# A decoder layer on one core: the next FFN part's first gate block moves in front of the down projections

## The chip, the cores and the metric

The kernel runs on one core of one Trainium2 chip. The metric is the device time of one launch in microseconds. The engines are named as in the profile: PE (TensorE matmul) with its weight loads PEld, DVE (VectorE), ACT (ScalarE), POOL (GpSimd) and SP (SyncE, which here only issues DMAs).

## The reference

One decoder layer over 256 tokens with model width 2048, all in float32. Two token mixers (retention and RG-LRU), a gated merge, a cross-attention over 256 memory tokens, and then the part that this change concerns:

```python
def conv_gated_ffn(hn, w_up, conv_w, conv_b, w_down):
    up = causal_dwconv(hn @ w_up, conv_w, conv_b)     # w_up: 2048 x 11264, 3 taps along the tokens
    gate, val = jnp.split(up, 2, axis=-1)
    return (jax.nn.silu(gate) * val) @ w_down         # w_down: 5632 x 2048
...
hn = rmsnorm(h, norm_ffn_w[l])
h = h + conv_gated_ffn(hn, ffn_w_up[l], ffn_conv_w[l], ffn_conv_b[l], ffn_w_down[l])
return rmsnorm(h, final_norm_w)
```

## The kernel before

**Matmuls in split float32.** Every operand is the sum of a rounded part `hi` and a remainder `lo`. A weight piece of 512 x 512 (1 MB, the tile `raw`, six buffers) is loaded by a DMA that SP issues; ACT writes `hi` (line 286), DVE writes `lo` (line 287), three buffers each. Three products (hi·hi, hi·lo, lo·hi) make one. One such piece is a *unit*: `units` yields the units in the order of `weight_plan`, and prepares each two units ahead (`AHEAD`).

**Three forms of a matrix product.** `gemm_n` has the tokens on the output's partitions: per unit 24 matmuls of 512 columns (lines 362, 363, 369), four units for an inner dimension of 2048. `gemm_t` has the features on the output's partitions: per unit 16 matmuls of 512 columns and 16 of 256 (line 351). `pair_products` makes two output blocks of 512 columns at once in 11 units with sums of operands (a Strassen-like scheme): seven units `q1` to `q7` of 12 matmuls and four units `p0` to `p3` of 24, in the order q1 p0 q3 p1 q5 q2 q6 p2 q7 q4 p3. Units q5 and q7 take their weights by a DMA of POOL that adds in place. `pair_add` adds the results to the residual rows `hrow`; its `out` is called after each unit.

**Callbacks.** `later(n, fn)` runs `fn` after the unit numbered n from here (0 is the next one) in the program's order. A scheduler then places the instructions on the engines' queues by priority and by buffers that are free; an engine works off its own queue in order.

**The FFN.** The 11 feature blocks of 512 are done in three parts of 4, 4 and 3 (`FF_PARTS`). In a part each block has two products, a gate block and a value block; `up` makes one. With `at` given it takes `gemm_n` and turns the result by DMA: ACT copies the accumulator into 16-bit planes (`row_planes`, line 757), two transposing DMAs of SP turn them (`turn_planes`, line 778), and at the two steps in `at` ACT joins the planes (line 763), DVE scales (line 1301), and `conv` does the three taps (ACT line 1311, DVE line 1313). With `at` None it takes `gemm_t`, whose result needs no turning. After the value block `hidden` makes silu(gate) times value and splits it (lines 1384 to 1386, 555, 556) into the operands `hid` of the down projection. The last value block of each part is made by `gemm_t`, and its conv and `hidden` run inside the first units of the down projection that follows. The down projection of a part of four blocks is two calls of `pair_add` (columns 0 and 1, then 2 and 3); unit p2 is the first that reads the last block's `hid`.

**Space.** The pool `bp` has 24 buffers of 4 KB per partition (`big`): the eight operands `h2s` of the FFN, up to eight `hid` and four sums of them, gate and value tiles `fg` and `fv`, planes `rp` and `d`, and the residual rows. The four residual row blocks are kept in DRAM (`fkept`) while a part's up products run, and `get_rows` brings them back: blocks 0 and 1 in the last value block, 2 and 3 in the first pair of the down projection.

**rsb.** `spread_tokens` spreads the reciprocal norms over the partitions with four small matmuls (line 605); `rsb2` is first read when the first gate block of the FFN has been turned.

Of the kernel before, what the change touches and what calls it, by code (L numbers as in the profile page):

```python
# [9 lines left out]
F32 = mybir.dt.float32  # L10
# [7 lines left out]
P = 128  # L18
# [46 lines left out]
def weight_plan():  # L65

    w0 = "w_in"
    plan = []
    v, u = O_V, O_V + 1024
    plan += [(w0, 0, NT, O_Q), (w0, 0, NT, v), (w0, 0, NT, O_K), (w0, 0, NT, v + BW), (w0, 0, NT, O_G, O_G + BW)]  # L70
    plan += [(w0, 0, NT, O_Q + BW), (w0, 0, NT, u, u + BW), (w0, 0, NT, O_K + BW)]
    plan += [(w0, 0, NT, O_G + 1024, O_G + 1024 + BW)]
    for b in range(4):
        plan += [(w0, 0, NT, c + b * BW) for c in (O_XR, O_YR)]
    for w, c, pairs in ((w0, O_GA, (0, 2)), (w0, O_GB, (0,)), ("w_proj_ret", 0, (0, 2))):
        plan += [(w, 0, NT, c + b * BW, c + (b + 1) * BW) for b in pairs]
        if len(pairs) == 1:
            plan += [(w, 0, NT, c + b * BW) for b in (2, 3)]
    plan += [("w_proj_rnn", 0, NT, b * BW) for b in range(4)]
    plan += residual_plan("w_mix_out")  # L80
    plan += [(w, 0, NT, b * BW, (b + 1) * BW) for w in ("xa_w_q", "xa_w_k") for b in (0, 2)]
    plan += residual_plan("xa_w_v")
    plan += residual_plan("xa_w_o")
    b0 = 0
    for nb_ in FF_PARTS:
        for b in range(b0, b0 + nb_):
            plan += [("ffn_w_up", 0, NT, c + b * BW) for c in (0, FF)]
        if nb_ == 4:
            plan += [("ffn_w_down", b0 * BW, NT, b * BW, (b + 1) * BW) for b in (0, 2)]
        else:  # L90
            plan += [("ffn_w_down", b0 * BW, 4 * nb_, b * BW) for b in range(4)]
        b0 += nb_
    return plan
# [61 lines left out]
def hybrid_layer(  # L155
# [265 lines left out]
            with tc.high_priority(URGENT):  # L421
                out(kind, x, z, yu, rw)

    def pair_add(w, row, st, ss, c0, c1, h0, h1):

        def add(o, i, op=ALU.add):
            dve.tensor_tensor(out=o, in0=o, in1=i, op=op)  # L427

        def out(kind, x, z, yu, rw):
            if kind == "q1":  # L430
                add(h0[:, 0, :], x)
            elif kind == "q5":
                later(3, lambda: add(h1, rw))
                later(4, lambda: add(h1, z[:, None, :].to_broadcast([P, 2, BW])))
            elif kind == "q6":
# [664 lines left out]
    def residual(w, st, ssum, out, osum, wcol, steps=None):  # L1100

        ss = sp_.tile([P, 2, 4], F32, tag="ss0", name=nm("ss"))
        for bs in RESIDUAL[w]:
            if steps:
                steps(bs[0])
            if len(bs) > 1:
                pair_add(w, 0, st, ssum, bs[0] * BW, bs[1] * BW, hrow[bs[0]], hrow[bs[1]])
            else:
                h = hrow[bs[0]]
                dve.tensor_add(h, h, gemm_n(w, 0, st, NT, bs[0] * BW))  # L1110
# [174 lines left out]
    h2s = []  # L1285
    ss2 = residual("xa_w_o", osp, osp_sums, h2s, None, p_ffn)
    rs2 = rstd_rows(ss2)
    later(1, lambda: spread_tokens(rs2))


    def up(c0, b, at, then):
# [89 lines left out]
    def hidden(gt, vl, pr, summed):  # L1381
# [6 lines left out]
        if summed and len(hid_sums) < KC:  # L1388
            hid_sums.append(sums(o, 0.5))

    put_rows(0, range(4))
    b0 = 0
    for part, nb_ in enumerate(FF_PARTS):
# [3 lines left out]
        for b in range(b0, b0 + nb_):  # L1397
            gt, vl = big([P, 4, S], s="fg"), big([P, 4, S], s="fv")
            last = b + 1 == b0 + nb_
            up(0, b, (1, 2), lambda pr, z, b=b, gt=gt: conv(0, b, pr, z, gt))  # L1400
            if last:
                later(0, lambda part=part, n=2 if paired else 4: get_rows(part % 2, range(n)))

            def finish_up(pr, z, b=b, gt=gt, vl=vl, paired=paired):
                conv(FF, b, pr, z, vl)
                hidden(gt, vl, pr, paired)

            if last and paired:
                for pr, a in enumerate(gemm_t("ffn_w_up", 0, h2s, NT, FF + b * BW)):
                    later(1 + 2 * pr, lambda pr=pr, z=scaled(a, "uz"): finish_up(pr, z))  # L1410
            else:
                up(FF, b, None if last else (1, 2), finish_up)
        if final:
            wfin = []
            for i in range(2):
# [6 lines left out]
        if nb_ == 4:  # L1422
            for b in (0, 2):
                if b == 0:
                    later(8, lambda part=part: get_rows(part % 2, (2, 3)))
                pair_add("ffn_w_down", b0 * BW, hid, hid_sums, b * BW, (b + 1) * BW, hrow[b], hrow[b + 1])
                put_rows((part + 1) % 2, (b, b + 1))
        else:
            for b in range(4):
# [37 lines left out]
```

## Time and profile before

| | |
|---|---|
| median of three runs | 1982.5 us (1980.45 to 1986.23) |
| profiled execution, own time | 1983.02 us |
| its span | 1981.2 us |
| granted TensorE clock, mean | 0.998 |
| busy: PE / DVE / ACT | 99% / 79% / 65% |

The span is the time from the first to the last instruction in the trace; the own time has the launch around it. "Busy" PE counts pipelined matmuls, so a slow stretch can also be busy. A row of the timeline has its start, its length, engine, line, operation and tiles, and in brackets the idle time before it with what ended that. A row of the windows has a stretch, its length, and the busy time of each engine in it with the number of instructions, then the granted clock, the share of DMA time and GB/s.

### The profile page before, as it was taken

What the parts mean: (1) busy time and instruction counts of PE and PEld (TensorE: products, weight loads), DVE (VectorE), ACT (ScalarE), POOL (GpSimd) and SP (SyncE); (2) the same over time, 40 slices, a digit from 0 to 9 for tenths busy, and PEclk for the clock granted to TensorE, in tenths of its full rate; (3) what the DMA queues carried; (4) which work ended last, traced back from release to release, by engine and by line L of the source; (5) the groups of instructions that cost most, each with busy time, mean ns of one, the idle gap of its engine ahead of it and who ended that gap; (6) DMA issues with size and microseconds to landing.
All of it is one profiled execution on the core that took longest, in us unless ns stands there. A gap on an engine that the chain in (4) does not pass through costs nothing.

```text
span 1981.2 us, 23716 instructions
## 1 busy us (share of the span) xinstructions
PE 1963.0 (99%) x9328; PEld 1647.8 (83%) x9328; DVE 1567.7 (79%) x1550; ACT 1289.3 (65%) x1341; POOL 43.3 (2%) x52
## 2 busy tenths in 40 slices
PE   9999999999999999999999999999999999999998
PEld 7888888888888888888888888888878888888887
DVE  6988887889986876779888768777797776986775
ACT  6655656768667656667878757667754676646653
POOL 0000000000000000000000000000000000000000
PEclk9999999999999999999999999999999999999999
DMA  9675674655887876878999739767777677786771
GB/s 372 232 258 148 232 262 163 217 204 144 269 261 222 255 255 195 265 272 247 274 256 234 285 112 272 269 211 223 212 247 269 204 222 242 216 296 211 216 242 63
DMA packets 152799, 458.16 MB, mean 231 GB/s; under 512 B 84080, under 2 KB 88816, under 8 KB 104944
## 3 DMA queue, kind: packets, MB, share of 16 engines
q1 hardware_dynamic: 145408, 412.08, 60.0%
q0 software_dynamic: 5760, 41.95, 11.7%
q10 hardware_dynamic: 1520, 2.63, 0.4%
q8 instruction: 73, 1.20, 0.2%
q14 instruction: 38, 0.31, 0.0%
HBM read 420.96 MB, written 16.78 MB: 221 GB/s over the span
## 4 chain that ended last, share of the span: by engine, by line
PE 79%; DVE 8%; DMA 5%; issue 4%; ACT 4%; SPq 1%; POOLq 0%; POOL 0%; ACTq 0%; DVEq 0%
PE acc L363 21%; PE acc L362 21%; PE acc L369 20%; PE acc L351 13%; DVE lo L287 4%; DMA raw<-in_wall 3%; ACT hi L286 2%; PE sm L518 2%; DMA d<-rp 1%; PE acc L518 1%; PE sm L964 1%; DVE raw L294 1%; SPq L778 1%; DVE fv L1313 1%; ACT jp L763 1%
## 5 line engine op out<-in xcount | busy, mean ns | idle before, releaser
L287 DVE TENSOR_TENSOR lo<-raw,hi 128x2048 fp32r<-128x2048 f32 (+1 forms) x420 | 951.6, 2269 | 281.4 <-ACT hi L286 278.2
L286 ACT CAST hi<-raw 128x2048 fp32r<-128x2048 f32 (+1 forms) x418 | 792.5, 1901 | 470.6 <-PE acc L363 311.0
L362 PE MATMUL acc<-hi,s 128*128 128x512 f32 x1944 | 758.9, 390 | 3.8 <-ACT s L555 3.8
L363 PE MATMUL acc<-hi,s 128*128 128x512 f32 x1944 | 757.8, 390 | 0.5 <-DVE s L556 0.5
L369 PE MATMUL acc<-lo,s 128*128 128x512 f32 x1944 | 485.5, 389 | 0.0
L362 PEld LDWEIGHTS acc<-hi,s 128*128 128x128 f32 x1944 | 365.2, 188 | 80.0 <-ACT s L555 5.1
L363 PEld LDWEIGHTS acc<-hi,s 128*128 128x128 f32 x1944 | 365.4, 188 | 76.4 <-DVE s L556 1.3
L369 PEld LDWEIGHTS acc<-lo,s 128*128 128x128 f32 x1944 | 365.3, 188 | 75.9
L351 PE MATMUL acc<-s,hi 128*128 128x512 f32 x960 | 230.6, 392 | 1.6 <-DVE hi L284 0.8
L351 PEld LDWEIGHTS acc<-s,hi 128*128 128x128 f32 x960 | 177.2, 188 | 37.4 <-ACT hi L286 1.4
L763 ACT COPY jp<-d 128x512 uint16<-128x512 uint16 x144 | 102.3, 771 | 42.3 <-DMA d<-rp 42.3
L351 PEld LDWEIGHTS acc<-s,lo 128*128 128x128 f32 x960 | 123.2, 191 | 5.4 <-DVE lo L287 1.3
L351 PE MATMUL acc<-s,lo 128*128 128x256 f32 x960 | 126.8, 284 | 0.5 <-DVE lo L287 0.5
L362 PE MATMUL acc<-hi,ss 128*128 128x512 f32 x320 | 125.7, 393 | 1.1 <-ACT o L454 0.6
L363 PE MATMUL acc<-hi,ss 128*128 128x512 f32 x320 | 124.7, 390 | 0.0
L369 PE MATMUL acc<-lo,ss 128*128 128x512 f32 x320 | 85.6, 389 | 0.0
L362 PEld LDWEIGHTS acc<-hi,ss 128*128 128x128 f32 x320 | 60.1, 188 | 15.7 <-issue 1.6
L369 PEld LDWEIGHTS acc<-lo,ss 128*128 128x128 f32 x320 | 60.1, 188 | 12.6
L363 PEld LDWEIGHTS acc<-hi,ss 128*128 128x128 f32 x320 | 60.1, 188 | 12.2
L267 POOL DMA_DIRECT2D raw<-in_wall x40 | 35.3, 881 | 1538.9 <-DVE lo L287 916.3
L427 DVE TENSOR_TENSOR nat<-nat,acc 128x512 f32<-128x512 f32 (+1 forms) x49 | 44.1, 911 | 5.0 <-PE acc L369 3.2
L292 DVE TENSOR_TENSOR raw<-raw,raw 128x2048 f32<-128x2048 f32 x20 | 45.8, 2290 | 0.4
(232 smaller groups left out, 1252.8 us busy)
## 6 DMA issues: line engine op xcount, KB each, us to landing
raw<-in_wall SPq DMA_DIRECT2D x333, 1024.0 KB, 5.1
raw<-in_wall POOLq DMA_DIRECT2D x40, 1024.0 KB, 8.5
fkept<-nat SPq DMA_DIRECT2D x12, 512.0 KB, 7.8
nat<-fkept SPq DMA_DIRECT2D x12, 512.0 KB, 4.9
xt<-in_x_t SPq DMA_DIRECT2D x11, 256.0 KB, 7.8
raw<-in_wall SPq DMA_DIRECT2D x5, 512.0 KB, 8.0
nat<-in_x ACTq DMA_DIRECT2D x4, 512.0 KB, 10.1
ret<-hr SPq DMA_DIRECT2D x4, 512.0 KB, 4.4
```

Source lines behind the costliest of these rows:

```text
L267: pool.dma_start(out=raw, in_=src, accum_op=ALU.add)
L286: act.copy(hi[:, a:b], raw[:, a:b])
L287: dve.tensor_tensor(out=lo[:, a:b], in0=raw[:, a:b], in1=hi[:, a:b].bitcast(F32), op=ALU.subtract)
L292: dve.tensor_tensor(out=to, in0=to, in1=by, op=ALU.add)
L294: dve.tensor_tensor(out=raw, in0=raw, in1=held["B"], op=ALU.add)
L351: pe.matmul(a, part, sx, start=k == 0 and t == 0, stop=k == nk - 1 and t == 0, skip_group_check=True)
L362: pe.matmul(o, h, hi, start=start and kk == 0, stop=False, skip_group_check=True)
L363: pe.matmul(o, l, hi, start=False, stop=False, skip_group_check=True)
L369: pe.matmul(o, h, lo, start=False, stop=stop and kk == KC - 1, skip_group_check=True)
L427: dve.tensor_tensor(out=o, in0=o, in1=i, op=op)
L518: ins = pe.matmul(o, a, b, start=start and i == 0, stop=stop and i == 2, skip_group_check=True)
L763: ins = act.copy(words(t)[:, :, :, 1 - i], d[:, i, 2 * pr : 2 * pr + 2, :])
```

## The change

1. The gate block of the next part's first feature block is computed after a part's last value block and before its down projections (`next_gate`). It is turned at steps 3 and 4 of the first pair, its conv is done there, and the result is stored to DRAM (`gkept`, 512 KB). The next part loads it instead of computing it.
2. With a gate block behind them, the last value blocks of the first two parts are made by `gemm_n` and turned by DMA like the others, at steps 1 and 2 of that gate block. The third part keeps `gemm_t`.
3. Residual rows 0 and 1 are read back at step 2 of the down projection's first pair instead of in the last value block, and rows 2 and 3 at step 9 instead of 8. So that the pair doesn't need row 0 at once, its first add moves from unit q1 to unit q5 (`late`).
4. `spread_tokens` runs two units later (step 3 instead of 1).

```diff
@@ weight_plan
-            plan += [("ffn_w_up", 0, NT, c + b * BW) for c in (0, FF)]
+            plan += [("ffn_w_up", 0, NT, c + b * BW) for c in ((0, FF) if b > b0 or b == 0 else (FF,))]
+        if b0 + nb_ < sum(FF_PARTS):
+            plan += [("ffn_w_up", 0, NT, (b0 + nb_) * BW)]
@@ pair_add
-    def pair_add(w, row, st, ss, c0, c1, h0, h1):
+    def pair_add(w, row, st, ss, c0, c1, hs, late=False):
...
         def out(kind, x, z, yu, rw):
-            if kind == "q1":
+            h0, h1 = (hrow[i] for i in hs)
+            if kind == "q1" and not late or kind == "q5" and late:
                 add(h0[:, 0, :], x)
-            elif kind == "q5":
+            if kind == "q5":
                 later(3, lambda: add(h1, rw))
@@ before the FFN
-    later(1, lambda: spread_tokens(rs2))
+    later(3, lambda: spread_tokens(rs2))
@@ the FFN
+    gkept = dp.tile([len(FF_PARTS), P, 4, S], F32, name="gkept")
+
+    def next_gate(part, b):
+
+        gt = []
+
+        def then(pr, z):
+            if pr == 0:
+                gt.append(big([P, 4, S], s="fg"))
+            conv(0, b, pr, z, gt[0])
+            if pr == 1:
+                sp.dma_start(out=gkept[part], in_=gt[0])
+
+        up(0, b, (3, 4), then)
...
-            up(0, b, (1, 2), lambda pr, z, b=b, gt=gt: conv(0, b, pr, z, gt))
-            if last:
-                later(0, lambda part=part, n=2 if paired else 4: get_rows(part % 2, range(n)))
+            if b0 and b == b0:
+                sp.dma_start(out=gt, in_=gkept[part - 1])
+            else:
+                up(0, b, (1, 2), lambda pr, z, b=b, gt=gt: conv(0, b, pr, z, gt))
+            if last and final:
+                later(0, lambda part=part: get_rows(part % 2, range(4)))
...
-            if last and paired:
-                for pr, a in enumerate(gemm_t("ffn_w_up", 0, h2s, NT, FF + b * BW)):
-                    later(1 + 2 * pr, lambda pr=pr, z=scaled(a, "uz"): finish_up(pr, z))
-            else:
-                up(FF, b, None if last else (1, 2), finish_up)
+            up(FF, b, None if last and final else (1, 2), finish_up)
+        if not final:
+            next_gate(part, b0 + nb_)
+            later(2, lambda part=part: get_rows(part % 2, (0, 1)))
...
                 if b == 0:
-                    later(8, lambda part=part: get_rows(part % 2, (2, 3)))
-                pair_add("ffn_w_down", b0 * BW, hid, hid_sums, b * BW, (b + 1) * BW, hrow[b], hrow[b + 1])
+                    later(9, lambda part=part: get_rows(part % 2, (2, 3)))
+                pair_add("ffn_w_down", b0 * BW, hid, hid_sums, b * BW, (b + 1) * BW, (b, b + 1), b == 0)
```

More of the change, by code (lines that the diff above doesn't have):

```diff
@@ L1106, in residual @@
             if len(bs) > 1:
-                pair_add(w, 0, st, ssum, bs[0] * BW, bs[1] * BW, hrow[bs[0]], hrow[bs[1]])
+                pair_add(w, 0, st, ssum, bs[0] * BW, bs[1] * BW, bs)
             else:
```

## The prediction

> **What bounds the kernel now.** The page first, for which engine carries the time.
>
> ```profile
> PE 1963.0 (99%) x9328; PEld 1647.8 (83%) x9328; DVE 1567.7 (79%) x1550; ACT 1289.3 (65%) x1341; POOL 43.3 (2%) x52
> ```
>
> PE is the bound, so an edit is worth only what it takes from PE's own line: shorter matmul work, or a stretch where PE waits. Therefore I cut the end of the first FFN part and of the second into windows, at the places in PE's timeline where a product starts.
>
> ```profile
> core 0: us, PE busy (x) PEld busy (x) DVE busy (x) ACT busy (x) POOL busy (x), PEclk, DMA share, GB/s
> 1386.38:1408.14 21.76, 21.76 (x98) 18.02 (x96) 18.37 (x25) 18.27 (x21) 0.00 (x0) 1.00 0.60 195
> 1408.14:1430.36 22.22, 22.22 (x130) 19.68 (x129) 15.07 (x18) 14.24 (x17) 0.90 (x1) 1.00 0.75 220
> 1430.36:1475.18 44.82, 43.02 (x182) 34.85 (x181) 43.53 (x40) 26.57 (x21) 1.77 (x2) 0.96 0.74 233
> 1475.18:1515.98 40.80, 40.80 (x181) 33.78 (x180) 35.24 (x21) 20.98 (x12) 0.86 (x1) 1.00 0.86 275
> 1668.30:1690.52 22.22, 22.22 (x129) 19.67 (x128) 14.91 (x17) 14.37 (x17) 0.86 (x1) 1.00 0.72 223
> 1690.52:1732.98 42.46, 41.65 (x183) 33.64 (x181) 41.25 (x38) 26.49 (x21) 1.76 (x2) 1.00 0.75 240
> ```
>
> In order: the last gate block of part 0 (`gemm_n`), its last value block (`gemm_t`), the two pairs of its down projection, then the last value block and the first pair of part 1. The gate block is the clean case: 96 matmuls in 21.76 us, 0.227 us each, nothing lost. A clean pair is 7 x 12 + 4 x 24 = 180 such matmuls, 40.80 us, and the second pair of part 0 takes just that. The first pairs take 44.82 and 42.46 us. PE's timeline shows where, in unit p2 of part 0:
>
> ```profile
> 1455.54 0.39 PE L363 MATMUL acc<-hi,s 128*128 128x512 f32 x1
> 1457.50 0.49 PE L362 MATMUL acc<-hi,s 128*128 128x512 f32 x1 [1.57 <-ACT s L555]
> 1458.22 0.50 PE L363 MATMUL acc<-hi,s 128*128 128x512 f32 x1 [0.23 <-DVE s L556]
> ...
> 1459.54 0.63 PE L362 MATMUL acc<-hi,s 128*128 128x512 f32 x1
> ...
> 1461.67 0.63 PE L363 MATMUL acc<-hi,s 128*128 128x512 f32 x1
> 1462.10 2.36 PE L369 MATMUL acc<-lo,s 128*128 128x512 f32 x8
> ```
>
> PE waits for the split of the last block's hidden operand: 1457.50 - 1455.54 - 0.23 = 1.7 us, then 0.5 us. Afterwards the six matmuls from 1459.54 to 1462.10 start 0.427 us apart, twice 0.227: the clock is halved for a while, as the 0.96 in the window's clock column says. That costs 6 x 0.2 us there and 0.4 us in the last row (2.36 us where eight matmuls at 0.227 take 7 x 0.227 + 0.39 = 1.98), 1.6 us together. Why the operand is late stands in the rows of ACT and DVE:
>
> ```profile
> 1455.02 1.90 ACT L286 CAST hi<-raw 128x2048 fp32r<-128x2048 f32 x1 [4.33 <-DMA raw<-in_wall]
> 1456.82 0.62 ACT L555 ACTIVATE s<-fo 128x512 fp32r<-128x512 f32 x1
> ```
>
> ```profile
> 1450.53 0.69 DVE L1385 SCALAR_TENSOR_TENSOR fo<-ft,fg 128x512 f32<-128x512 f32 x1
> 1451.13 2.29 DVE L287 TENSOR_TENSOR lo<-raw,hi 128x2048 fp32r<-128x2048 f32 x1
> 1453.33 0.69 DVE L1386 TENSOR_TENSOR fo<-fo,fv 128x512 f32<-128x512 f32 x1
> ```
>
> The product of gate and value is ready only at 1454.02, because DVE is full (43.53 of 44.82 us), and then its split stands behind a `hi` cast that waits on ACT for a weight DMA.
>
> The Trainium skill, "TensorE: Matmul & The Clock Gate", section "What's actually happening", says that the array's clock is halved after an idle window of about 3.4 us. The trace agrees on the halving and not on the length: 2.2 us of waiting were enough here, and the other first pair, with less waiting, has a clock of 1.00. If by that rule the half-rate stretch were no consequence of the wait, its 1.6 us would stay, and the sum below would be smaller by them.
>
> **The change part by part.** *The gate block in front.* It does for PE what it did in the next part: 21.76 us, moved. What it buys is 21.76 us between the last value product and the down projection. Conv and `hidden` of that value then run beside a gate block, which is what the first window shows for an inner block: DVE 18.37 and ACT 18.27 of 21.76 us, PE without loss. So p2 finds its operand some 30 us old, and the excess goes: 44.82 - 40.80 = 4.02 us in part 0, 42.46 - 40.80 = 1.66 us in part 1.
>
> *Last values by token.* Twice `gemm_t` becomes `gemm_n`: 2 x (22.22 - 21.76) = 0.92 us of pure PE work. It costs other engines, per block, from these groups and transfers:
>
> ```profile
> L757 ACT COPY rp<-acc 128x1024 uint16<-128x1024 uint16 x38 | 36.3, 1007 | 0.0
> L763 ACT COPY jp<-d 128x512 uint16<-128x512 uint16 x144 | 102.3, 771 | 42.3 <-DMA d<-rp 42.3
> L1301 DVE TENSOR_TENSOR jp<-jp,rsb 128x512 f32<-128x512 f32 x38 | 25.9, 689 | 24.7 <-ACT jp L763 24.5
> L1313 DVE SCALAR_TENSOR_TENSOR fg<-jp,pf,fg 128x255 f32<-128x255 f32 (+1 forms) x88 | 38.5, 481 | 6.5 <-ACT fg L1311 5.4
> ```
>
> ```profile
> raw<-in_wall SPq DMA_DIRECT2D x333, 1024.0 KB, 5.1
> ...
> fkept<-nat SPq DMA_DIRECT2D x12, 512.0 KB, 7.8
> nat<-fkept SPq DMA_DIRECT2D x12, 512.0 KB, 4.9
> ...
> d<-rp SPq DMA_TRANSPOSE x56, 4.0
> ```
>
> ACT gets 2 x 1.01 + 4 x 0.77 = 5.1 us and loses two accumulator copies, DVE loses two adds, SP gets two transposes. The block in which this lies is then an inner block, so the first window is its price: nothing.
>
> *The gate's turning and conv inside the first pair.* New there on DVE: 2 x 0.69 + 8 x 0.48 = 5.2 us, on top of the 35.24 us of the clean pair: 40.4 of 40.80 us. This is the tightest place. From the pair's start the units begin at q1 0, p0 2.7, q3 8.2, p1 10.9, q5 16.3, q2 19.0, q6 21.8, p2 24.5, q7 29.9, q4 32.6, p3 35.4 us; a q unit needs its `lo` 1.8 us after its start, a p unit 3.6 us. Laid in a row on DVE from `lo` of q2 at 15.0 with 2.2 us a piece: 17.2; first half of the gate 19.6; late add of row 0 20.2; `lo` of q6 22.4 (due 23.6); second half 24.8; an add 25.4; `lo` of p2 27.6 (due 28.1); the sum for q4 29.8; `lo` of q7 32.0 (due 31.7). Before, with the value's work there, `lo` of q6 ended at 1453.42, 23.1 us into the pair, also in time. I take 0.3 us a part, 0.6 us in all; the ends are 0 (the schedule of before, no row shows a gain beyond the clean pair) and 2.7 us a part (what DVE's 43.53 us before had over 40.80).
>
> *Buffers and SP.* At step 2 the 24 buffers hold 8 `h2s`, 8 `hid`, 4 sums, `rp` and `d`: two are left, for rows 0 and 1. That this pool is full in this place before, too, shows in SP's rows:
>
> ```profile
> 1412.73 4.85 SPq L778 DMA_TRANSPOSE d<-rp  x2
> ...
> 1418.78 20.62 SPq L265 DMA_DIRECT2D raw<-in_wall  x3
> 1451.28 3.10 SPq L1379 DMA_DIRECT2D nat<-fkept  x2
> 1456.25 12.81 SPq L265 DMA_DIRECT2D raw<-in_wall  x5
> ```
>
> The first row block is issued at 1451.28, just when line 1385 has read the gate tile for the last time (1450.53 + 0.69 = 1451.22), the second just after line 1386 (1454.02). With the change rows 0 and 1 go out at about 11 us and land 4.9 us later, before q5 ends at 19.0 and well before q6 at 21.8, whose matmuls must not overwrite the accumulator that the late add reads. The gate tile takes over `rp`: the transposes of the last gate were over 1412.73 + 4.85 - 1408.14 = 9.4 us after its product, landed by 13, and the tile is first written at 16. The stores of the gate wait on SP for the conv, with weight loads queued behind; between 1439.40 and 1456.25 SP had no weight load to issue, 9.0 to 25.9 us into the pair, so the store (ready at about 25) costs nothing. Without that hole it delays the next load, which at 25.9 + 5.1 = 31.0 would land 4.4 us ahead of its unit, p3. The load of the kept gate and the second pair of rows, at step 9, have free buffers. DMA, at a share of 0.74 in this window, gets 2.0 MB more (two rows, the gate, one turning), which its 0.86 in the second pair leaves room for.
>
> *`spread_tokens` later.*
>
> ```profile
> 1268.47 0.39 PE L362 MATMUL acc<-hi,s 128*128 128x512 f32 x1
> 1269.53 0.68 PE L605 MATMUL sm<-diag,ones 128*128 128x128 f32 x4 [0.67 <-DVE s L579]
> ```
>
> PE loses 1269.53 - 1268.47 - 0.23 = 0.83 us here, behind the splits that still read the small accumulators. Two units later these are long done; `rsb` is read two units after that. What it can cost is a wait behind one `lo`, 0 to 2.3 us; I take 0.
>
> **Sum:** 4.02 + 1.66 + 0.92 + 0.83 - 0.6 = 6.8 us. Against the profiled execution's own 1983.0 us this gives 1976.2; that execution is 0.5 us above the median of the three runs, so the forecast for the median is 1982.5 - 6.8 = 1975.7 us. A measurement can tell about 0.3%, 5.9 us here, as much as the three runs are apart: faster means below 1976.6, slower above 1988.4.
>
> **The rivals.** *DVE takes it back.* The gate's conv replaces the value's, DVE stays at 99% in the first pairs, and `lo` of q6 or q7 comes late. For it: 40.4 of 40.80 us. Against it: the same amount lay there before and only p2's operand was late. Price: up to 2.7 us a part; about half of it, 1.3 us each, gives 1982.5 - 7.4 + 2.6 = 1977.7, the whole 1980.5.
>
> *Slower: the rows come too late.* If two buffers are missing at step 2, rows 0 and 1 wait for `d`, which is free only after the second half's join at about 22 us, and land at 27. The late add then holds DVE's queue, with `lo` of q6 and p2 behind it, and q6 starts at 27.7 instead of 21.8: 5.9 us, and after such a wait 1.6 us of half clock as above, 7.5 a part. 1982.5 - 7.4 + 15 = 1990.1. It decides from a landing later than 21 us on. The Trainium skill, "TensorE: Matmul & The Clock Gate", section "Architectural detail", calls the queues of ACT and DVE strictly first in, first out, which speaks against an add that waits for a DMA; the split behind the cast at 1455.02 agrees. Against the rival: the count of buffers, and 10 us between issue and need where 4.9 are used.
>
> *It doesn't do what it says.* If the wait in p2 only moves to another operand of the same pair, 0.92 + 0.83 us remain: 1980.7.
>
> **How the numbers follow.** Forecast 0.58; DVE takes it back 0.20; no removal 0.07; slower 0.15. The forecast's case lies below 1976.6 four times in five, and the mild end of the second adds a little: faster 0.50, slower 0.15, the same 0.35. The range goes from the forecast less the 2.1 us by which the lowest run is under the median and the 0.6 us allowance, 1973.0, to 1983.5, which is the third case with most of the spread of the runs upwards; the slower case is left out.
>
> **What would show it.** Right: first pairs of 40.8 to 41.4 us, clock 1.00 there, no wait for ACT line 555 in p2; two value blocks of 21.76 us; no wait at line 605. The wait of about 2 us for line 555 in the third part's down projection stays. Wrong: q6 or q7 waiting for DVE line 287 or for the add of line 427 behind a row's DMA; `hi` casts waiting for `raw`; SP's row loads issued after 16 us in the pair.

## The result, and the profile after

The changed kernel takes 1978.4 us in the median of twelve runs (1976.9 to 1980.2), the kernel before 1982.9 us beside it (twelve runs, 1980.4 to 1990.4). The ratio is 0.9971, with a 95% interval from 0.9963 to 0.9978: 4.6 us faster, where 6.8 were forecast. That lies inside the forecast's range (1973.0 to 1983.5 us), but not below the 1976.6 us that it called faster. A good part of the gain comes from a place that the forecast had left out, and the largest term of the sum was mostly lost again.

The profiled execution of the changed kernel took 1980.2 us, its span is 1978.4 us. The page of the changed kernel, busy time of the engines:

```profile
PE 1960.3 (99%) x9264; PEld 1643.0 (83%) x9264; DVE 1564.5 (79%) x1546; ACT 1294.5 (65%) x1349; POOL 43.2 (2%) x52
```

Nothing in this line tells what happened; it takes the stages. The windows of the changed kernel, with the columns of before: the last value block of part 0, the gate block now in front, the two pairs of part 0, then the first pair of part 1.

```profile
1409.03:1430.79 21.76, 21.76 (x97) 18.02 (x96) 16.07 (x19) 14.52 (x16) 0.00 (x0) 1.00 0.70 220
1430.79:1452.55 21.76, 21.76 (x97) 18.02 (x96) 16.37 (x19) 15.54 (x18) 0.90 (x1) 1.00 0.76 200
1452.55:1495.76 43.21, 41.49 (x181) 33.55 (x180) 37.32 (x31) 27.83 (x23) 1.76 (x2) 1.00 0.82 275
1495.76:1536.56 40.80, 40.80 (x181) 33.78 (x180) 36.32 (x21) 20.86 (x12) 0.86 (x1) 1.00 0.90 284
1710.64:1753.60 42.96, 41.23 (x182) 33.56 (x181) 36.89 (x30) 27.73 (x23) 1.76 (x2) 1.00 0.81 271
```

The value block by token takes 21.76 us instead of 22.22, as forecast, and the gate block in front loses nothing. The first pairs take 43.21 and 42.96 us, not 40.8 to 41.4: part 0 gained 1.6 us, and part 1 lost 0.5 us against its 42.46. DVE is less busy there than forecast (37.3 us, not 40.4), so it isn't simply full. PE's timeline of the changed kernel in the first pair of part 0 (all line numbers after the added lines are two or three higher than before; 362, 363, 369 have become 364, 365, 371):

```profile
1474.64 0.47 PE L364 MATMUL acc<-hi,ss 128*128 128x512 f32 x1 [0.17 <-DVE nat L429]
...
1481.11 1.97 PE L371 MATMUL acc<-lo,s 128*128 128x512 f32 x8
1484.63 0.50 PE L364 MATMUL acc<-hi,s 128*128 128x512 f32 x1 [1.54 <-ACT hi L288]
...
1485.44 0.50 PE L364 MATMUL acc<-hi,ss 128*128 128x512 f32 x1
```

The wait in p2 is gone: the eight `lo` matmuls at 1481.11 are its last ones, with nothing lost ahead of them. After it PE could have gone on at 1482.92 (1481.11 + 8 x 0.227). It goes on at 1484.63 with three matmuls of q4, and with q7, the next unit in the program, at 1485.44 (`ss` marks operands that are sums; q7 has them, q4 doesn't). The row blames ACT, for q4's `hi`. But q4 stands there only because the scheduler put it ahead of q7, and q7 was not ready either. DVE and ACT of the changed kernel, in the same stretch:

```profile
1475.02 2.28 DVE L289 TENSOR_TENSOR lo<-raw,hi 128x2048 fp32r<-128x2048 f32 x1
1478.62 1.76 DVE L1316 SCALAR_TENSOR_TENSOR fg<-jp,pf,fg 128x255 f32<-128x255 f32 x4 [1.32 <-ACT fg L1314]
1480.30 2.28 DVE L294 TENSOR_TENSOR raw<-raw,raw 128x2048 f32<-128x2048 f32 x1
1482.51 2.28 DVE L289 TENSOR_TENSOR lo<-raw,hi 128x2048 fp32r<-128x2048 f32 x1
1484.71 0.68 DVE L429 TENSOR_TENSOR nat<-nat,acc 128x512 f32<-128x512 f32 x1
```

```profile
1476.17 1.92 ACT L288 CAST hi<-raw 128x2048 fp32r<-128x2048 f32 x1 [2.49 <-DMA raw<-in_wall]
1477.99 1.09 ACT L1314 ACTIVATE fg<-jp,pf 128x256 f32<-128x256 f32 x2
1482.68 3.71 ACT L288 CAST hi<-raw 128x2048 fp32r<-128x2048 f32 x2 [3.59 <-DVE raw L294]
```

Units q6 and q7 use the same accumulator, so q7 may begin only when line 429 has taken q6's result out of it and into its row, at 1484.71 + 0.68 = 1485.39; q7 begins at 1485.44. That add is the last of a queue. Ahead of it stand the second half of the gate's conv (line 1316), q4's sum (line 294) and q7's `lo` (line 289). And the conv itself began late: DVE stands for 1.32 us until ACT has done line 1314, which stands behind q7's `hi` cast, which has waited 2.49 us for the DMA that adds q7's weights in place. Of the 2.5 us by which q7 is late (1485.44 - 1482.92), 1.3 are DVE standing and 1.2 are work ahead of the add.

This add was just as late before, which the forecast had not seen. In part 0 of before it is this row of DVE:

```profile
1462.49 0.68 DVE L427 TENSOR_TENSOR nat<-nat,acc 128x512 f32<-128x512 f32 x1
```

It ends 32.8 us into the pair (1463.17 - 1430.36), as in the changed kernel (1485.39 - 1452.55 = 32.8). There PE had lost 4 us in p2 by then, so nothing waited for it. In the other three first pairs of before's two executions, where less was lost in p2, q7 starts 0.05 to 0.06 us after the end of this add. DVE had stood 1.26 us for p2's late split there, so a part of this lateness came from p2 itself; the rest was a second wait, which the one in p2 hid.

The waits of PE over the FFN's last 600 us, in the second execution of the changed kernel (e11) and in the second one of before (e12); the columns are engine, line, releaser, us in total, times, and the longest.

```profile
PE acc L364 <- ACT hi L288: 3.2, 2, 1.7
PE acc L364 <- DVE nat L429: 0.4, 1, 0.4
PE acc L364 <- ACT s L558: 0.2, 1, 0.2
...
PE acc L362 <- ACT s L555: 3.8, 3, 1.8
PE acc L363 <- DVE s L556: 0.4, 2, 0.2
```

The first three rows are the changed kernel: the same two waits ahead of q7, one in each part, the small one at q6, and a short one in the third part's down projection. The last two are before: p2 in two parts, and the third part's down projection.

That third wait is the unpredicted gain. The forecast said that it stays. The last turning of the third part and its wait, first before, then changed (SP's issue of the two transposing DMAs, ACT's join that waits for them, PE's first matmul on the last split):

```profile
1885.65 5.27 SPq L778 DMA_TRANSPOSE d<-rp  x2
1894.51 2.03 ACT L763 COPY jp<-d 128x512 uint16<-128x512 uint16 x3 [6.20 <-DMA d<-rp]
1920.27 0.73 PE L362 MATMUL acc<-hi,s 128*128 128x512 f32 x2 [1.69 <-ACT s L555]
...
1884.51 4.96 SPq L781 DMA_TRANSPOSE d<-rp  x2
1891.61 2.03 ACT L766 COPY jp<-d 128x512 uint16<-128x512 uint16 x3 [4.44 <-DMA d<-rp]
1917.38 0.73 PE L364 MATMUL acc<-hi,s 128*128 128x512 f32 x2
```

From issue to join it was 8.9 us and is 7.1 us. From start to start, less a matmul's 0.227 us, PE lost 1.85 us here before (1.67 in its second execution) and loses 0.1 us now (0.3). By the trace's landing times the very last transposing DMA takes 7.3 to 7.5 us in the two executions of before and in e6, and 5.7 to 6.0 us in every other kernel run here. Those three are the executions whose parts 0 and 1 keep `gemm_t` for the last value block. Code and order of the third part are the same in all of them.

What differs is another transfer. The page of each kernel lists a queue q8 of the kind `instruction`, with 73 transfers in before and in e6 and 72 in the kernels with the token form, which have 64 fewer matmuls (9264 in the changed kernel, 9328 before). To within half a microsecond, one of these transfers falls 5.7 to 5.8 us after the issue of the third part's last turning in before, in its second execution and in e6, while the turning is in flight; in the eleven others the next one comes only after 14.7 to 17.1 us. Two other places of the FFN bear this out. At the turning near 1842 us it is the other way round: the eleven have the transfer beside it and take 7.3 to 7.6 us, the three have none and take 5.7 to 6.1 us. At the one near 1634 us the three have it again (7.2 to 7.5 us, against 5.8 to 6.0). So the last turning was late where an instruction transfer ran beside it, and the change moved that transfer elsewhere. No run here moved it alone, so the cause is read from the traces, not shown.

One more thing is needed to read single profiles. In code that no kernel here touched, ahead of the FFN, PE waits differently in each execution (at about 1040 us 1.7 us in the changed kernel's first profile, nothing in its second, 0.6 us in before's second). So I compare the stretch from the first transpose ahead of the FFN's up products to the end, called the FFN below:

| kernel | FFN, us | first pair, part 0 | part 1 |
|---|---|---|---|
| before, first and second execution | 723.2, 721.9 | 44.8, 43.6 | 42.5, 42.3 |
| changed, first and second execution | 718.9, 719.0 | 43.2, 43.4 | 43.0, 43.0 |

### The profile page after: what moved, and what is told of

Read it like the earlier page. It is cut to its first block, busy times and chain, and to the rows that moved or that the text cites. A ratio compares the mean times of both kernels' runs of the same rounds, so it can differ in the third digit from the quotient of the medians.

```text
span 1978.4 us, 23613 instructions
## 1 busy us (share of the span) xinstructions
PE 1960.3 (99%) x9264; PEld 1643.0 (83%) x9264; DVE 1564.5 (79%) x1546; ACT 1294.5 (65%) x1349; POOL 43.2 (2%) x52
## 4 chain that ended last, share of the span: by engine, by line
PE 87%; DVE 4%; DMA 3%; issue 2%; ACT 2%; SPq 0%; POOLq 0%; ACTq 0%; DVEq 0%; POOL 0%
PE acc L364 23%; PE acc L365 23%; PE acc L371 23%; PE acc L353 14%; DMA raw<-in_wall 3%; DVE lo L289 2%; PE sm L521 2%; ACT hi L288 2%; PE acc L521 1%; DVE raw L296 1%; PE sm L967 1%; PE sm L535 0%; DVE tb L725 0%; DVE nat L429 0%; DVE raw L294 0%
## 5 line engine op out<-in xcount | busy, mean ns | idle before, releaser
L364 PE MATMUL acc<-hi,s 128*128 128x512 f32 x2008 | 783.1, 390 | 3.3 <-ACT hi L288 3.3
L365 PE MATMUL acc<-hi,s 128*128 128x512 f32 x2008 | 781.6, 389 | 0.0
L371 PE MATMUL acc<-lo,s 128*128 128x512 f32 x2008 | 500.9, 389 | 0.0
L364 PEld LDWEIGHTS acc<-hi,s 128*128 128x128 f32 x2008 | 376.9, 188 | 81.8 <-ACT hi L288 4.1
L371 PEld LDWEIGHTS acc<-lo,s 128*128 128x128 f32 x2008 | 376.8, 188 | 78.2
L365 PEld LDWEIGHTS acc<-hi,s 128*128 128x128 f32 x2008 | 377.0, 188 | 77.6 <-DVE s L559 0.2
L353 PE MATMUL acc<-s,hi 128*128 128x512 f32 x832 | 200.4, 392 | 1.5 <-DVE hi L286 1.3
L353 PEld LDWEIGHTS acc<-s,hi 128*128 128x128 f32 x832 | 153.5, 188 | 32.3 <-issue 1.6
L766 ACT COPY jp<-d 128x512 uint16<-128x512 uint16 x152 | 108.4, 771 | 40.1 <-DMA d<-rp 40.1
L353 PEld LDWEIGHTS acc<-s,lo 128*128 128x128 f32 x832 | 107.0, 191 | 4.9 <-DVE lo L289 1.3
L353 PE MATMUL acc<-s,lo 128*128 128x256 f32 x832 | 110.5, 284 | 0.5 <-DVE lo L289 0.5
```

The source lines that it names most:

```text
L353: pe.matmul(a, part, sx, start=k == 0 and t == 0, stop=k == nk - 1 and t == 0, skip_group_check=True)
L364: pe.matmul(o, h, hi, start=start and kk == 0, stop=False, skip_group_check=True)
L365: pe.matmul(o, l, hi, start=False, stop=False, skip_group_check=True)
L371: pe.matmul(o, h, lo, start=False, stop=stop and kk == KC - 1, skip_group_check=True)
L766: ins = act.copy(words(t)[:, :, :, 1 - i], d[:, i, 2 * pr : 2 * pr + 2, :])
```

## The experiments

The expectations name the theories by letter. **A**, the chain: q7's release stands in in-order queues behind something that waits (DVE for ACT's line 1314, this behind a cast, this for a DMA), and PE's own order, q4 ahead of q7, adds to it. **B**, the amount: the gate's conv and the late add are simply too much DVE work ahead of q7. **C**: q7's weights land later than before, because the pair has more traffic. C fell by the traces alone: POOL issues the adding DMA 15.4 us into the pair and it lands at 23.5 us; before, it was 16.5 and 24.5 us.

**e1, the gate's turning later.** The conv moves out of the crowded stretch, to steps 7 and 8.

```diff
-        up(0, b, (3, 4), then)
+        up(0, b, (7, 8), then)
```

> The gate block's turning and conv run at steps 7 and 8 of the first pair instead of 3 and 4. In the changed kernel the first pairs take 43.2 and 42.9 us where 40.8 is clean, with one wait of 1.7 and 1.9 us for the hi cast of unit q4, whose first matmuls stand ahead of q7 on PE. Theory A (a chain of queues: the sum that q4 reads stands on DVE behind the second half of the gate's conv, which waits for ACT behind q7's cast, which waits for POOL's adding DMA): the conv is then behind that sum, the wait goes, pairs of 40.8 to 41.3 us, 3 to 4.5 us faster than the changed kernel. Theory B (DVE has 40 of 40.8 us of work in the pair, so something is late in any order): pairs stay above 42.3 us, with a wait for another operand; less than 1 us gained. Theory C (the weights that POOL adds for q7 land later because of the added transfers): the wait stays as it is.

Measured: 1988.4 us, ratio 1.0019 (1.0004 to 1.0034). The wait ahead of q7 is gone from the first pairs (41.37 us in part 0), so it is with the conv ahead of it that q7 is late. But the second pairs lose 4.4 and 7.3 us, with waits of up to 2.3 us each and half clock after the longest. ACT and SP of e1 show where they come from:

```profile
1506.72 3.72 ACT L288 CAST hi<-raw 128x2048 fp32r<-128x2048 f32 x2 [10.13 <-DMA raw<-in_wall]
```

```profile
1487.58 0.33 SPq L267 DMA_DIRECT2D raw<-in_wall  x1
...
1492.12 0.33 SPq L1405 DMA_DIRECT2D gkept<-fg  x1
...
1495.02 0.32 SPq L1419 DMA_DIRECT2D fg<-gkept  x1
1496.49 0.33 SPq L267 DMA_DIRECT2D raw<-in_wall  x1
```

Between 1487.58 and 1496.49 SP loads no weights: stores, a row and the gate's load fill its queue. ACT then stands 10.1 us for a weight piece. (That the one causes the other is read from the order of the queue; no run took it apart.) The forecast had priced that queue at nothing for the changed kernel, where a hole hides it; a few units later there is no hole.

**e2, q7 first on PE.** q4's first matmuls are tied behind q7's, so that PE keeps the program's order (`pin` is true in unit q4 of a first pair).

```diff
-            pe.matmul(o, h, hi, start=start and kk == 0, stop=False, skip_group_check=True)
+            ins = pe.matmul(o, h, hi, start=start and kk == 0, stop=False, skip_group_check=True)
+            if pin and kk == 0:
+                tc.keep_in_program_order(ins)
```

> Only the order on PE is pinned: in the first pair of a part q4's first matmuls stay behind q7, as written. Theory A: q7 starts on time, since its cast ended at 1478.1 and PE was free at 1482.9; the lo of q7 ends at 1484.8, 0.1 us after q7 needs it, and q4's cast at 1484.6, before q4. Pairs of 40.8 to 41.5 us, about 3 us faster than the changed kernel. Theory B: the wait moves to the lo of q7 and keeps 1.2 us or more. Theory C: q7 itself waits for its cast, 1.7 us.

Measured: 1983.6 us, ratio 1.0005 (0.9984 to 1.0026); the pairs take 46.18 and 45.18 us. PE of e2, at q7 (line 431 is 429 of the changed kernel):

```profile
1482.71 0.47 PE L364 MATMUL acc<-hi,ss 128*128 128x512 f32 x1 [2.42 <-DVE nat L431]
...
1484.24 0.63 PE L364 MATMUL acc<-hi,ss 128*128 128x512 f32 x1
1484.67 0.63 PE L367 MATMUL acc<-hi,ss 128*128 128x512 f32 x1
```

Now the row names the true releaser, the add of line 429, and q7 waits 2.6 us in each part; then the clock halves (0.43 us from one matmul to the next). So the part of A that blames PE's order falls: q4 ahead of q7 saved time.

**e3, the gate kept unturned.** The gate goes to DRAM as 16-bit planes straight from the accumulator; the next part turns it with its loading DMA and does the conv at steps 2 and 3 of its value block. All of it leaves the pair.

```diff
-    gkept = dp.tile([len(FF_PARTS), P, 4, S], F32, name="gkept")
+    gkept = dp.tile([len(FF_PARTS), S, 2 * BW], U16, name="gkept")
@@ next_gate
...
-        up(0, b, (3, 4), then)
+        t = row_planes(gemm_n("ffn_w_up", 0, h2s, NT, b * BW))
+        sp.dma_start(out=gkept[part].rearrange("(t p) c -> p t c", p=P), in_=t.rearrange("p t a w -> p t (a w)"))
+    def kept_gate(part, b, gt):                 # called where the kept gate was loaded
+        d = big([P, 2, KC, S], U16, s="d")
+        sp.dma_start_transpose(out=d.rearrange("p a c s -> p (a c) s"), in_=gkept[part])
+        def turned(pr):
+            z = join_planes(d, pr)
+            dve.tensor_tensor(out=z, in0=z, in1=rsb2, op=ALU.mult)
+            conv(0, b, pr, z, gt)
+        for pr in range(2):
+            later(2 + pr, lambda pr=pr: turned(pr))
```

> The gate block in front is stored to DRAM as 16-bit planes straight from the accumulator, and turned, joined and convolved in the next part beside its first value block, where DVE was busy 10.3 and ACT 7.7 of 21.8 us before. Nothing of it is left in the first pair but two ACT copies and one store. Theories A and B: pairs of 40.8 us, 4 to 4.5 us faster than the changed kernel, about 1974. Theory C: the same store of 512 KB stays and the wait too.

Measured: 1974.8 us, ratio 0.9946 (0.9925 to 0.9968). The windows of e3, the gate block in front and the first pair of part 0, and the first pair of part 1:

```profile
1429.27:1451.03 21.76, 21.76 (x97) 18.02 (x96) 16.28 (x19) 15.53 (x18) 0.90 (x1) 1.00 0.76 200
1451.03:1491.97 40.94, 40.94 (x182) 33.72 (x180) 35.13 (x21) 23.43 (x15) 1.76 (x2) 1.00 0.87 285
1706.85:1747.76 40.91, 40.91 (x181) 33.71 (x180) 34.60 (x20) 23.20 (x15) 1.76 (x2) 1.00 0.84 278
```

Both pairs are what the forecast had promised, and PE's waits in them are gone. The FFN takes 714.7 us, 4.3 less than the changed kernel's: 2.3 and 2.1 us in the two first pairs. With e10 it is the fastest kernel run here, by some 9 us in the median under the kernel before.

**e4, the conv's start on DVE.** The second half's scale and bias move from ACT to DVE. DVE gets 0.73 us more work and no longer stands for ACT. By A the wait shrinks; by B alone it would not.

```diff
@@ conv, for the second half of the gate in front
-            act.activation(y, z[:, j, :], AF.Identity, scale=pf[:, 2, t : t + 1], bias=pf[:, 3, t : t + 1])
+            dve.tensor_scalar(out=y, in0=z[:, j, :], scalar1=pf[:, 2, t : t + 1], scalar2=pf[:, 3, t : t + 1], op0=ALU.mult, op1=ALU.add)
```

> In the second half of the gate's conv the first step (scale and bias) moves from ACT to DVE; nothing else. Theory A: DVE's idle 1.3 us before that conv goes, two instructions of 0.3 to 0.5 us come, so the wait for q4's hi falls from 1.7 to about 1.1 us and from 1.9 to about 1.3. Theory B: DVE has 0.7 us more to do and the wait grows to about 2.4 us. Theory C: the wait stays 1.7 and 1.9 us.

Measured: 1976.7 us, ratio 0.9959 (0.9941 to 0.9977); the pairs take 42.47 and 41.86 us, the wait ahead of q7 is 0.88 and 0.89 us instead of 1.7 and 1.9, and the FFN takes 716.9 us, 2 us less than the changed kernel's. DVE of e4:

```profile
1476.93 2.28 DVE L289 TENSOR_TENSOR lo<-raw,hi 128x2048 fp32r<-128x2048 f32 x1
1479.13 0.73 DVE L1315 TENSOR_SCALAR fg<-jp,pf 128x256 f32<-128x256 f32 x2
1479.78 1.66 DVE L1322 SCALAR_TENSOR_TENSOR fg<-jp,pf,fg 128x255 f32<-128x255 f32 x4
1481.36 2.29 DVE L294 TENSOR_TENSOR raw<-raw,raw 128x2048 f32<-128x2048 f32 x1
```

There is no idle time in it any more. More work on DVE and less wait: the standing behind ACT is a real part of the cause. The rest of the wait stays.

**e5, the token form alone.** No gate in front, everything else as changed.

```diff
...
-        if b0 + nb_ < sum(FF_PARTS):
-            plan += [("ffn_w_up", 0, NT, (b0 + nb_) * BW)]
...
-            next_gate(part, b0 + nb_)
```

> Of the change only the last value blocks by token remain (with the rows back later and spread_tokens later); the gate block stays in the next part. Theory A (the gate block in front is what takes the wait out of p2, since the value needs a product's time to be turned): in the changed kernel the second split of the value ends 24.4 us into the gate block; inside a down pair, whose DVE is fuller, it comes at 27 to 30 us, p2 starts at 24.5, so p2 waits 3 to 6 us and runs at half clock for a while: first pairs of 45 to 48 us where before took 44.8 and 42.5, the kernel 1 to 7 us slower than before. Rival (the token form itself brings the gain): faster than before by 3 us or more.

Measured: 1992.5 us, ratio 1.0044 (1.0025 to 1.0063), slower than expected; the pairs take 50.7 and 48.5 us. PE of e5, in p2:

```profile
1458.68 0.80 PE L362 MATMUL acc<-hi,s 128*128 128x512 f32 x1 [5.33 <-ACT s L556]
```

The last value is now also turned inside the pair, and p2 waits 5.5 us for its split, with the half clock after it. This is the wait that the gate block in front removes: the changed kernel and e6, which keeps `gemm_t`, have a gate block there and no wait in p2. The forecast's reading of it was right.

**e6, the gate in front alone.** The last values of parts 0 and 1 by `gemm_t`, as before.

```diff
-            up(FF, b, None if last and final else (1, 2), finish_up)
+            if last and paired:
+                for pr, a in enumerate(gemm_t("ffn_w_up", 0, h2s, NT, FF + b * BW)):
+                    later(2 * pr, lambda pr=pr, z=scaled(a, "uz"): finish_up(pr, z))
+            else:
+                up(FF, b, None if last else (1, 2), finish_up)
```

> The gate block in front as in the changed kernel, but the last value blocks of parts 0 and 1 by feature as before (gemm_t), their conv at steps 0 and 2 of the gate block. Theory A: two blocks of 22.2 instead of 21.8 us, 0.9 us lost, first pairs unchanged at 42.9 to 43.2 us; about 0.9 us slower than the changed kernel. Rival (turning one more block by DMA costs ACT and SP what the form saves): the same time as the changed kernel or less.

Measured: 1984.9 us, ratio 1.0001 (0.9982 to 1.002), where 0.9 us over the changed kernel was expected; its FFN takes 723.6 us, 4.6 more than the changed one's. ACT and DVE of e6 in the first pair, which starts at 1452.40:

```profile
1461.57 0.77 ACT L766 COPY jp<-d 128x512 uint16<-128x512 uint16 x1 [5.20 <-DMA d<-rp]
```

```profile
1464.15 2.29 DVE L289 TENSOR_TENSOR lo<-raw,hi 128x2048 fp32r<-128x2048 f32 x1 [5.45 <-ACT hi L288]
```

The join waits 5.2 us for the turning DMA (2.8 us in the changed kernel), the next cast stands behind it, DVE stands behind the cast, and q6 then starts 1.9 us late, before the wait of 1.7 us ahead of q7 comes as well. In part 1 q6 is only 0.3 us late. And the third part's wait of 1.7 us is back. Here too an instruction transfer runs beside the late turning: it comes 3.9 us after the issue, and the two DMAs land after 5.6 to 6.0 us; in the changed kernel none comes within 10 us, and they land after 3.2 to 3.3. So of the 4.6 us only the 0.9 of the two `gemm_t` blocks belong to the form itself; some 3 us more lie in the two places where a turning was late. In the medians neither half of the change gains anything alone (e5 10 us slower, e6 nothing); together they give 4.6 us.

**e7, the rows early.** Rows 0 and 1 are back in the gate block, and the first add is at q1 again: one add less in the crowded stretch.

```diff
+            if last and not final:
+                later(0, lambda part=part: get_rows(part % 2, (0, 1)))
...
-            later(2, lambda part=part: get_rows(part % 2, (0, 1)))
...
-                pair_add(..., (b, b + 1), b == 0)
+                pair_add(..., (b, b + 1))
```

> Rows 0 and 1 are read back at step 0 of the gate block in front, and row 0's first add is back at unit q1; the rest as in the changed kernel. Theory A (DVE stands idle 1.3 us in the first pair for ACT, which waits for POOL's DMA): the add of 0.6 us leaves the stretch ahead of that idle time, which grows by as much; the wait ahead of q7 stays 1.7 and 1.9 us and only the 0.3 us at q6 goes. Theory B (DVE's amount of work): the wait ahead of q7 falls to 1.1 and 1.3 us.

Measured: 1977.0 us, ratio 0.997 (0.9949 to 0.9992); pairs of 42.25 and 42.27 us, the wait ahead of q7 1.33 and 1.39 us, between what A and B expected and nearer to B. The small wait at q6 is gone, another of 0.6 us in the second pair of part 0 has come, and the FFN takes 718.2 us, 0.8 less than the changed kernel's. DVE of e7:

```profile
1475.10 2.28 DVE L294 TENSOR_TENSOR raw<-raw,raw 128x2048 f32<-128x2048 f32 x1
1477.31 1.66 DVE L1316 SCALAR_TENSOR_TENSOR fg<-jp,pf,fg 128x255 f32<-128x255 f32 x4
1478.89 2.28 DVE L289 TENSOR_TENSOR lo<-raw,hi 128x2048 fp32r<-128x2048 f32 x1
1481.09 0.68 DVE L429 TENSOR_TENSOR nat<-nat,acc 128x512 f32<-128x512 f32 x1
```

The scheduler used the time freed to put q4's sum ahead of the conv, where DVE stood before; neither theory had reckoned with that. So here DVE does not stand ahead of the conv, and the wait that is left, 1.3 us, is work ahead of the add: the other half of the cause.

**e8, `spread_tokens` early again.**

```diff
-    later(3, lambda: spread_tokens(rs2))
+    later(1, lambda: spread_tokens(rs2))
```

> Only spread_tokens is back at step 1. Forecast of the prediction: PE waits 0.8 us at the small matmuls again. Rival, from the trace of the changed kernel, where PE waited 0.36 us for the same splits one block of transposes earlier: the wait belongs to the splits of the last rows and only changes its place, so the first product of the FFN is 0.3 to 0.5 us longer, not 0.8.

Measured: 1982.9 us in one run, its FFN 719.2 us against 718.9 and 719.0 of the changed kernel. The wait of 0.9 us at line 608 (605 of before) is back. In the changed kernel's first profile the same splits hold up the second group of transposes ahead of the FFN (line 535) by 0.36 us instead, in its second they don't. All that PE loses between 1255 and 1330 us is 1.4 and 1.5 us in before, 1.5 in e8, 0.9 and 0.6 in the changed kernel: the step is worth 0.5 to 0.8 us, a little less than the 0.83 forecast and more than the rival's reading of a wait that only moves. The FFN as a whole differs by 0.2 to 0.3 us only, so the size rests on that stretch.

**e9, the add first.** As e2, and the add of q6's result with a higher priority, so that it goes ahead of the sum and the `lo`.

```diff
-            with tc.high_priority(URGENT):
+            with tc.high_priority(200 if pinned and kind == "q6" else URGENT):
```

> As the run that pinned q7 ahead of q4, and in addition the add that empties q7's accumulator (the out of unit q6, 0.7 us on DVE) moves ahead of the sum and the lo that stood before it, 4.5 us of DVE work. Nothing is taken away. Theory A2 (q7 waits for this add, because it stands behind other work on DVE's queue): q7 starts on time, is held at most 0.7 us by its own lo, and q4's cast is ready: first pairs of 41.3 to 42.0 us where the changed kernel takes 43.2 and 42.9; about 2.5 us faster than the changed kernel. Theory B (DVE's amount of work in the pair): another lo or cast is late instead, and the pairs stay at 42.5 us or more.

Measured: 1977.7 us, ratio 0.9969 (0.9957 to 0.9981), pairs of 42.19 and 41.89 us. PE of e9:

```profile
1481.56 0.39 PE L364 MATMUL acc<-hi,ss 128*128 128x512 f32 x1
...
1484.06 1.19 PE L373 MATMUL acc<-lo,ss 128*128 128x512 f32 x4 [0.52 <-DVE lo L289]
```

The pairs lie at the upper end of what A2 expected, one of them between A2 and B. q7 starts without a gap after p2 (1479.75 + 8 x 0.227 = 1481.56), so the add was its release. Then its `lo` matmuls are 0.7 us late, 0.95 us in part 1, and two waits of 0.3 and 1.4 us appear in the second pairs. Reordering one queue moves the lateness on; the FFN, 718.6 us, is hardly shorter than the changed kernel's.

**e10, e3 and e7 together.**

```diff
+    ...                                  (the edit of e3)
...                                       (get_rows as in e7)
-                pair_add(..., (b, b + 1), b == 0)
+                pair_add(..., (b, b + 1))
```

> The gate block kept unturned, as in the run that kept 16-bit planes in DRAM, and rows 0 and 1 read back at step 0 of that gate block with row 0's add at q1. With the pairs clean at 40.8 us already there is nothing left to gain: the same time within 1 us of that run, about 1974.5. Rival (the late add and the late rows still cost something): more than 1 us faster than it.

Measured: 1975.6 us, ratio 0.9957 (0.9945 to 0.9969); pairs of 40.8 us, FFN 714.6 us. That is e3's result: with the conv out of the pair it no longer matters when the rows come.

**e11, the changed kernel again, and e12, the kernel before again**, without an edit, to have a second profile of each.

> The changed kernel once more, to compare it on this chip with the two others and to see which waits of its profile come back. The waits ahead of q4's first matmuls (1.7 and 1.9 us) are in the order of the queues and come back; the wait of 1.7 us before the FFN and the short one in the third part's down projection are of transfers' landing and may be another length, up to 2 us each.

> The kernel before once more, for its profile. Its first trace has a wait of 1.8 us in the third part's down projection, which the changed kernel's two traces have at 0.1 and 0.3 us; program and order are the same there. If the wait is of the transfers' landing in one execution, it comes at another length, below 1 us; if the change took it away, it comes back at 1.5 to 2 us. The waits in p2 (4.0 and 1.7 us lost) and at the small matmuls (0.8 us) are in the order of the queues and come back within 0.3 us.

Measured: e11 1979.3 us, ratio 0.997 (0.9951 to 0.9989), in the same comparison as e10, which is 3.7 us under it; the FFNs, 719.0 and 714.6 us, say 4.4. e12: 1981.4 us in one run. PE of e12 in p2 of part 0:

```profile
1457.48 0.50 PE L362 MATMUL acc<-hi,s 128*128 128x512 f32 x1 [1.79 <-ACT s L555]
1458.21 0.50 PE L363 MATMUL acc<-hi,s 128*128 128x512 f32 x1 [0.22 <-DVE s L556]
...
1460.88 1.98 PE L369 MATMUL acc<-lo,s 128*128 128x512 f32 x8
```

The same wait as in the forecast's rows, even a little longer, and no half clock after it: the eight matmuls take 1.98 us, not 2.36. The third part's wait came back at 1.67 us, so by the expectation the change took it away, and it wasn't one execution's chance.

## Why the prediction was right or wrong

Each term, as forecast and as the two executions of each kernel have it (minus is a gain):

| term | forecast, us | measured, us |
|---|---|---|
| first pair of part 0, with its allowance | -3.7 | -0.2 to -1.6 |
| first pair of part 1, with its allowance | -1.4 | +0.5 to +0.7 |
| last values by token | -0.92 | -0.92 |
| `spread_tokens` | -0.83 | -0.5 to -0.8 |
| third part's wait for the last split | 0 | -1.4 to -1.8 |
| sum | -6.8 | -2.3 to -4.6 |

The FFN as a whole gives -2.9 to -4.3 us, the medians -4.6.

**The step that failed** is the list of DVE's work in the first pair, with the 0.3 us a part that came out of it, and with it the term "the excess goes", 4.02 and 1.66 us. The list held each `lo` against its `lo` matmuls (q7's due at 31.7) and left out that q7's *first* matmul, due at 29.9, must wait for the add that reads q6's result. It has an add at 25.4, which can only be this one, since q6 ends at 24.5; the queue had it last, behind q4's sum and q7's `lo`, and it ended at 32.8 us. It had ended there before, too. So "only p2's operand was late", which the forecast held against the case "DVE takes it back", was a misreading: with the wait in p2 gone, the one behind it came out. The second error is that the list laid DVE's work end to end, with no standing for ACT, while 1.3 us of standing lay in it. That its end of q7's `lo` agrees (32.0 us, and 1484.79 - 1452.55 = 32.2 in the trace) is partly luck, as the list has the add ahead of that `lo`, where the trace has the standing.

To name DVE as the tightest place was right, but the reason given, its amount of 40.4 of 40.8 us, was not: the trace has 37.3. In size the case "DVE takes it back" came nearest: it priced 1977.7 us for 1.3 us a part and 1980.5 for 2.7, and the pairs took 2.4 and 2.2 us over the clean 40.80 (1.7 and 1.9 of it ahead of q7, the rest at q6 and in short gaps).

The Trainium skill, "TensorE: Matmul & The Clock Gate", section "Architectural detail", has the queues of ACT and DVE strictly first in, first out; the trace agrees, as an add of 0.68 us stood behind 6.3 us of other work (lines 1316, 294 and 289). The forecast had used that rule for the rows only, not for q6's result.

**The half clock.** 1.6 us of the 4.02 came from a half-rate stretch after the wait, taken as part of it. In e12 the same wait has none, so some 1.2 us of the term (44.8 - 43.6) belonged to that one execution.

**What held.** The wait in p2 had the cause named and went where the gate block came in front (also in e6; e5 has it at 5.5 us without that block). The value blocks took 21.76 us. The rows came in time: SP of the changed kernel issues them 5.7 us into the pair, behind the transposes.

```profile
1455.59 2.62 SPq L781 DMA_TRANSPOSE d<-rp  x2
1458.26 1.05 SPq L1382 DMA_DIRECT2D nat<-fkept  x2
...
1480.45 0.32 SPq L1405 DMA_DIRECT2D gkept<-fg  x1
```

So the slower case fell: q6 waits 0.3 us in part 0 (0.5 in the second execution) for an add of line 429, where 5.9 us would have been its price, and no add of a row stands for a row's DMA. The store at 1480.45 has no weight load waiting behind it, as worked out; e1 suggests what it costs elsewhere.

**What was missed.** "The wait of about 2 us in the third part stays" was wrong; it went, without a line of code there being changed. By e6, where it stays, and e5, where it goes, it goes with the token form of the earlier parts' last values and not with the gate in front. By the traces the form goes with another place of an instruction transfer, which nothing in the code of the third part shows; as far as the forecast goes, this gain is luck.

That the total came within 3 us of the forecast is luck in part: the first pairs kept 4.6 us over clean where 0.6 was allowed, some 1.2 us of the forecast's gain were one execution's half clock, and a gain of some 1.5 us that was not in the sum made up for a part of this.

## What to carry to other kernels

When work is moved into a stretch, list for each engine's queue not only how long the work takes but for whom each item is the release, and when that one is due: an add of 0.7 us that frees an accumulator held PE here nearly as long as the late split of p2 had. When a wait is to be taken away, look in the trace of before for what starts right at the end of something else behind it; this is the next wait. The product of the gate block hid well between two others, its follow-up work did not: e3 stores the raw result, does that work where the result is used, and its FFN is another 4.3 us shorter. And two halves of a change can each be worth nothing or cost 10 us alone; look in the traces for why before one is dropped, since some 3 us of what e6 lacks lie at two late transfers.

## What the runs showed of the hardware that was not expected

**After waits of 2 to 3 us the half clock came in some cases and not in others.** Waits of PE of up to 1.9 us in the FFN were never followed by half rate here. Of those between 2.2 and 2.6 us some were and some not: 2.2 us yes and 2.45 us no in the same unit of the same kernel (before, first and second execution), 2.3 us yes and 2.2 us no in e1, 2.6 us yes twice in e2. After 5.3 us and more (e5) it came both times. A half-rate stretch cost some 1.5 us in before, e1 and e2, and 1.6 and 2.3 us in e5. The Trainium skill, "TensorE: Matmul & The Clock Gate", section "What's actually happening", says that the window watched is free-running, which would fit the mixed outcomes; its length of about 3.4 us is more than what was enough here.

**A transposing DMA landed late where an instruction transfer ran beside it.** Take the turnings from 1320 to 1960 us of the fourteen traces whose two DMAs are issued within 1.8 us. Where an instruction transfer came 2.5 to 5.5 us after the second one's issue, this landed after 7.2 to 7.7 us in 31 of 33 cases (the other two took 4.8 and 5.6 us). Without one it took 3.1 to 6.2 us, with one exception (7.6 us, in the changed kernel near 1590 us). PE's wait behind the third part's last turning follows this: at most 0.4 us without such a transfer, 1.7 to 1.85 us with one. That the one causes the other is not shown.
